# One gate for the tensor engine's visits to half-height tiles in a two-mixer decoder layer

## The chip, the cores and the metric

The kernel runs on one core of a Trainium2 chip. The metric is the device time of one execution in microseconds; the kernel before took a median of 434.82 us in 3 runs (434.67 to 434.88). Lower is better. TensorE (PE) multiplies matrices, VectorE (DVE) and ScalarE (ACT) work elementwise, GpSimd (POOL) does a few adds, SyncE (SP) starts the transfers.

## The reference

One decoder layer on 512 tokens of width 1024. One input projection gives the inputs of two mixers, A (attention with three branches) and B (a gated linear recurrence of 4 heads); their outputs go through gates, two branch projections, an output projection and a layer norm:

```python
h = x @ w_in[l] + b_in[l]
(q_a, kv_a, g_nsa, z_a, q_b, f_b, i_b, z_b, gm_a, gm_b) = jnp.split(h, SPLIT_POINTS, axis=-1)
o_a = nsa_attention(q_a, k_cmp, v_cmp, k_slc, v_slc, k_win, v_win, g_nsa, ...)
o_a = o_a * jax.nn.silu(z_a)
o_b = hgrn2(q_b, f_b, i_b, lb_all[l])
...
y = jax.nn.sigmoid(gm_a) * (o_a @ w_branch_a[l]) + jax.nn.sigmoid(gm_b) * (o_b @ w_branch_b[l])
x = layer_norm(alpha * x + y @ w_out[l], ln_g[l], ln_b[l])
```

In the attention, per block of 128 queries: a branch on 31 compressed blocks, a branch on selected blocks (here all 8 blocks of 64 keys are selected, so it is causal attention on its own keys), and a window branch (512 wide, so again causal attention on its own keys). There are 8 query heads of 64 dimensions in 2 groups that share keys and values.

## The kernel before, in words

**Precision.** Every large product is made of three float32r products of split operands (hi x hi, hi x lo, lo x hi); `split2` (L153) makes the pair: ACT casts to the high part (L154), DVE subtracts to get the low part (L155).

**The long stream.** `proj` (L266) computes a 128-column tile of the input projection: 24 matmuls of 128x512 on a PSUM bank `pa`, from weight tiles `wraw` that are split into `whi` and `wlo` two tiles ahead. Before every sixth matmul it calls `weave.tick()`.

**The weave.** All the rest (recurrence, rotary keys and queries, the attention) is written as generators that run inside the ticks (`_Weave`, L74): a chain yields the number of ticks after which it goes on. `T.matmul`, `T.transpose` and the transfers keep program order, so the order in which the chains issue is the order on PE; a scheduler places ACT's and DVE's instructions. The table `D` (L70) holds the numbers of ticks.

**The attention of the selected and window branches.** `units` (L617) are (query block i, branches): (3, selected), (3, window), (2, selected), (2, window), (1, both), (0, both). For each unit `attn_scores` (L620) makes the scores of one head pair m at a time: the contraction is over 64 dimensions, so two matmuls run on the two halves of 64 rows of PE, each pair into two `pss` banks, three pairs per head pair (hi/lo). Then DVE adds the mask and takes the row maximum (L646), ACT exponentiates with the sum (L649). After four head pairs come reciprocals, gates and the multiplications of the probabilities (L661 on ACT, L663 on DVE). `attn_values` (L667) transposes the probabilities of the unit before, 16 transposes on half tiles of 64 rows into two `pst` banks, splits them (L154, L155) and issues the products with the values (four matmuls into `pso`) of the step before.

A **visit** below is a stretch of PE's order on half-height tiles between matmuls on all 128 rows: scores, transposes, or both in the same tick. Both chains start their visits on even ticks (L631 and L702):

```python
while weave.now % 2:
    yield 1
```

There are two banks each of `pa`, `pss`, `pst` and `pso`. The compressed branch uses `pst` for its transposes (`transpose4`, L595 and L612) and four banks, two of them `pst`, for its products with the values (L675, tiles of 32 rows). `hgrn` (L370) is the recurrence of one head; D["h6"] stands between its state update (L425, L428) and its output matmuls into `pso` (L431).

Of the kernel before, what the change touches and what calls it, by code (L numbers as in the profile page):

```python
# [12 lines left out]
AF = mybir.ActivationFunctionType  # L13
# [36 lines left out]
def _columns(name):  # L50

    c = np.arange(_COLS[name], _COLS[name] + 128)
    if name[0] == "q" and name[1] != "b" or name[:2] == "za":
# [13 lines left out]
    0, 128, 256, 384, 388, 900, 1412, 1924, 2436)  # L67


D = dict(h0=8, h2=4, h3=6, h4=2, h5=8, h6=5, n0=3, n1=2, n2=10, c0=1, c1=6, c2=7, c3=7,  # L70
         r0=5, p0=4, p1=11, p2=2, b0=1, a0=1, a1=1, a3=2, a4=2, a5=1, s0=18, s2=0, s3=1, a6=2)


class _Weave:  # L74


    def __init__(self):
        self.now, self.runs = 0, []

    def start(self, chain, delay=0):  # L80
        self.runs.append([chain, self.now + delay])
# [1 line left out]
    def tick(self):  # L83
        for run in list(self.runs):
            if run[1] <= self.now:
                wait = next(run[0], None)
                if wait is None:
                    self.runs.remove(run)
                else:
                    run[1] = self.now + wait  # L90
        self.now += 1

    def drain(self):
# [5 lines left out]
def layer_kernel(ctx: ExitStack, tc: tile.TileContext, xT, xn, w0, wi, wf, wv, small, brow, consts,  # L99
# [517 lines left out]
    units = [(i, brs) for i in range(3, -1, -1) for brs in (((0,), (1,)) if i >= 2 else ((0, 1),))]  # L617
    probs, pv_at = {}, [0]

    def attn_scores():  # L620
        while not {"keys0", "keys1", "gates"} <= ready or len(QAB) < 4:
            yield 1
        for u, (i, brs) in enumerate(units):
            while u - pv_at[0] > 1:
                yield 1
            n, nb = 128 * (i + 1), len(brs)
            mn, den, ts = SM(8 * nb, "mn"), SM(8 * nb, "dn"), ([], [])
            for m in range(4):
                while weave.now % 2:
                    yield 1  # L630

                pg = PS(), PS()
                qh, ql = (t[:, 128 * i:128 * i + 128] for t in QAB[m])
                for s, (q, k) in enumerate(((qh, KH), (qh, KL), (ql, KH))):
                    for ab in range(2):
                        r = slice(64 * ab, 64 * ab + 64)
                        if nb == 1:
                            dst, kk = pg[ab][:, 0:n], k[r, brs[0], 0:n]
                        else:
                            dst, kk = pg[ab][:, 0:2 * n].rearrange("p (b k) -> p b k", b=2), k[r, :, 0:n]  # L640
                        T.matmul(dst, q[r], kk, start=s == 0, stop=s == 2)
                for ab in range(2):
                    p = T2()
                    for x in range(nb):
                        c, k = slice(n * x, n * x + n), slice(4 * nb * ab + nb * m + x, 4 * nb * ab + nb * m + x + 1)
                        V.tensor_tensor_reduce(out=p[:, c], in0=pg[ab][:, c], in1=amask[:, 512 - n:512],  # L646
                                               op0=ALU.add, op1=ALU.min, scale=-0.125, scalar=3.0e38,
                                               accum_out=mn[:, k])
                        A.activation(p[:, c], p[:, c], AF.Exp, bias=mn[:, k], scale=-1.0, accum_out=den[:, k])  # L649
                    ts[ab].append(p)  # L650
                yield D["a6"]
            yield D["a0"]
            V.reciprocal(den, den)
            den3 = den.rearrange("p (h b) -> p h b", b=nb)
            V.tensor_tensor(den3, den3, gv[:, i, :, 1 + brs[0]:1 + brs[0] + nb], ALU.mult)
            for ab in range(2):
                for m in range(4):
                    for x in range(nb):
                        c, k = slice(n * x, n * x + n), slice(4 * nb * ab + nb * m + x, 4 * nb * ab + nb * m + x + 1)
                        if m % 2:  # L660
                            A.mul(ts[ab][m][:, c], ts[ab][m][:, c], den[:, k])  # L661
                        else:
                            V.tensor_scalar(ts[ab][m][:, c], ts[ab][m][:, c], den[:, k], None, ALU.mult)  # L663
                probs[u, ab] = ts[ab]

    def attn_values():
# [15 lines left out]
        for u, (i, brs) in enumerate(units):  # L682
            n, last = 128 * (i + 1), None
            while (u, 1) not in probs or len(vts) < 4:
                yield 1
            if brs[0] == 0:
                acc = PO(), PO()
                yield D["a1"]

            def products():  # L690

# [5 lines left out]
                        T.matmul(acc[ab], v, pts[k][:, ab], start=brs[x] == 0 and j == 0 and k == 0,  # L697
                                 stop=brs[x] == 1 and j == i and k == 1)

            for x in range(len(brs)):  # L700
                for j in range(i + 1):
                    while weave.now % 2:  # L702
                        yield 1


                    k = slice(n * x + 128 * j, n * x + 128 * j + 128)
                    pq = PT(), PT()
                    for ab in range(2):
# [9 lines left out]
                    if last:  # L718
                        products()
                    last = x, j, pts  # L720
                    yield D["a3"]
            pv_at[0] = u + 1
# [312 lines left out]
```

## Time and profile before

| what | value |
|---|---|
| median of 3 runs | 434.82 us |
| the profiled execution's own time | 435.02 us |
| its span in the trace | 432.9 us |
| PE matmul busy | 423.8 us (98%), 2381 instructions |
| DVE busy, ACT busy | 286.2 us (66%), 238.9 us (55%) |
| the chain that ended last | PE 91%, ACT 5%, DVE 2% |

The profiled execution is 0.20 us above the median. Matmuls are pipelined, so PE's busy share does not say how fast it goes: the distance between the starts of rows does. In a timeline row `x2` or `x16` counts matmuls of one form in a row, and "[0.27 <-ACT t L661]" is idle time before a row and what ended it.

### The profile page before, as it was taken

To read this page: it belongs to the slowest core of one execution; us is meant where nothing else is said; L and a number is where in the kernel's file an instruction comes from. 1 tells how busy PE (TensorE), PEld (TensorE's weight loads), DVE (VectorE), ACT (ScalarE), POOL (GpSimd) and SP (SyncE) were. 2 spreads that over 40 slices of the span, in tenths; PEclk is the share of its full clock that TensorE was granted. 3 is DMA by queue.
4 is the path that set the end of the run, shared out by engine and by line. 5 is a ranking of instruction groups with operands and counts; after the bars stand their busy time and mean duration, and the time that the engine had idled before them with its cause. 6 is when DMAs were issued, how large, how long until landed. Compare 5 with 4: busy or idle time off the path is not lost.

```text
span 432.9 us, 6424 instructions
## 1 busy us (share of the span) xinstructions
PE 423.8 (98%) x2381; PEld 344.8 (80%) x2381; DVE 286.2 (66%) x586; ACT 238.9 (55%) x484; POOL 15.6 (4%) x26
## 2 busy tenths in 40 slices
PE   8999999999999999999999999999999999999994
PEld 7888888888898878867677777776787888888884
DVE  5915669995556476955576556568664797872674
ACT  3534632623437345658777577769676875528300
POOL 2000000000001310000000010001000100000000
PEclk9999999999999999999999999999999999999999
DMA  8995400352420644321111211111252631153031
GB/s 263 393 374 185 166 1 2 85 145 86 123 76 3 188 145 151 97 99 51 48 50 56 81 59 51 51 48 50 73 192 82 218 106 62 50 149 144 15 130 48
DMA packets 20879, 47.58 MB, mean 110 GB/s; under 512 B 2929, under 2 KB 4593, under 8 KB 20849
## 3 DMA queue, kind: packets, MB, share of 16 engines
q1 hardware_dynamic: 20560, 46.92, 33.1%
q8 instruction: 18, 0.29, 0.3%
q10 hardware_dynamic: 288, 0.26, 0.2%
q14 instruction: 13, 0.10, 0.1%
HBM read 41.93 MB, written 2.10 MB: 102 GB/s over the span
## 4 chain that ended last, share of the span: by engine, by line
PE 91%; ACT 5%; DVE 2%; DMA 1%; issue 0%; DVEq 0%; ACTq 0%
PE pa L107 57%; PE pss L107 16%; PE pso L107 12%; PE pst L107 3%; PE pst L111 3%; ACT t L649 2%; ACT t L661 1%; ACT whi L154 1%; DMA t<-in_w_dram 1%; DVE t L155 1%; DVE wlo L155 1%; ACT asum L679 0%; DVE t L646 0%; ACT t L873 0%; ACT t L729 0%; ACT t L154 0%
## 5 line engine op out<-in xcount | busy, mean ns | idle before, releaser
L107 PE MATMUL pa<-t,whi 128*128 128x512 f32 x640 | 200.3, 394 | 0.0
L107 PEld LDWEIGHTS pa<-t,whi 128*128 128x128 f32 x640 | 118.2, 188 | 28.4 <-issue 3.1
L107 PE MATMUL pa<-t,wlo 128*128 128x512 f32 x320 | 124.9, 390 | 0.0
L155 DVE TENSOR_TENSOR wlo<-wraw,whi 128x1024 fp32r<-128x1024 f32 x46 | 56.5, 1231 | 41.0 <-ACT whi L154 41.0
L154 ACT CAST whi<-wraw 128x1024 fp32r<-128x1024 f32 x46 | 48.1, 1048 | 43.9 <-PE pa L107 27.9
L107 PEld LDWEIGHTS pa<-t,wlo 128*128 128x128 f32 x320 | 60.1, 188 | 12.8
L649 ACT ACTIVATE t<-t,sm_mn 128x512 f32<-128x512 f32 (+3 forms) x64 | 35.4, 555 | 26.6 <-DVE sm_mn L646 26.6
L107 PE MATMUL pa<-t,t 128*128 128x512 f32 (+1 forms) x168 | 36.7, 375 | 0.0
L155 DVE TENSOR_TENSOR t<-pst,t 128x512 fp32r<-128x512 f32 x40 | 25.9, 685 | 14.5 <-ACT t L154 14.5
L646 DVE CUSTOM_DVE_ANT_0 t<-pss,t 128x512 f32<-128x512 f32 (+3 forms) x64 | 28.4, 486 | 10.6 <-PE pss L107 8.9
L107 PEld LDWEIGHTS pa<-t,t 128*128 128x128 f32 x168 | 30.3, 188 | 5.6
L107 PE MATMUL pss<-t,t 128*128 128x512 f32 (+3 forms) x222 | 34.5, 310 | 0.0
L107 PE MATMUL pso<-t,t 128*128 128x512 f32 (+2 forms) x158 | 32.9, 343 | 0.2 <-DVE t L188 0.2
L107 PEld LDWEIGHTS pss<-t,t 128*128 128x128 f32 (+1 forms) x222 | 27.5, 175 | 3.7 <-issue 0.7
L107 PEld LDWEIGHTS pso<-t,t 128*128 128x128 f32 x158 | 25.2, 189 | 4.3 <-ACT t L187 0.5
L155 DVE TENSOR_TENSOR t<-t,t 128x512 fp32r<-128x512 f32 (+1 forms) x26 | 17.0, 669 | 16.4 <-ACT t L154 16.4
L154 ACT CAST t<-t 128x512 fp32r<-128x512 f32 (+1 forms) x26 | 15.2, 605 | 22.2 <-DVE t L901 14.8
L107 PE MATMUL pso<-t,vv 128*128 128x512 f32 x80 | 23.7, 417 | 0.0
L111 PEld LDWEIGHTS pst<-con,t 64*128 64x128 f32 (+1 forms) x349 | 16.8, 138 | 6.5 <-DVE t L155 1.7
L154 ACT CAST t<-pst 128x512 fp32r<-128x512 f32 x40 | 21.2, 577 | 0.7 <-PE pst L111 0.6
L111 PE MATMUL pst<-con,t 64*128 64x64 f32 (+1 forms) x349 | 19.6, 229 | 1.7 <-DVE t L663 0.8
L107 PE MATMUL pss<-t,whi 128*128 128x512 f32 x64 | 19.7, 389 | 0.0
(164 smaller groups left out, 501.0 us busy)
## 6 DMA issues: line engine op xcount, KB each, us to landing
wraw<-in_wf_dram SPq DMA_DIRECT2D x38, 512.0 KB, 3.7
wraw<-in_wbr_dram SPq DMA_DIRECT2D x8, 512.0 KB, 3.8
t<-in_wout_dram SPq DMA_DIRECT2D x16, 256.0 KB, 3.4
t<-in_w_dram SPq DMA_DIRECT2D x15, 256.0 KB, 5.6
t<-t SPq DMA_DIRECT2D x48, 64.0 KB, 2.0
t<-in_wi_dram SPq DMA_DIRECT2D x8, 256.0 KB, 6.0
t<-in_xn_dram SPq DMA_DIRECT2D x8, 256.0 KB, 6.6
out_dram<-t SPq DMA_DIRECT2D x8, 256.0 KB, 2.1
```

Of the source, the lines that this page charges most:

```text
L107: return tc.keep_in_program_order(nc.tensor.matmul(*a, **k))
L111: return tc.keep_in_program_order(nc.tensor.transpose(*a, **k))
L154: A.copy(dst_hi, src)
L155: V.tensor_tensor(dst_lo, src, dst_hi.bitcast(F32), ALU.subtract)
L646: V.tensor_tensor_reduce(out=p[:, c], in0=pg[ab][:, c], in1=amask[:, 512 - n:512], op0=ALU.add, op1=ALU.min, scale=-0.125, scalar=3.0e38, ...
L649: A.activation(p[:, c], p[:, c], AF.Exp, bias=mn[:, k], scale=-1.0, accum_out=den[:, k])
L661: A.mul(ts[ab][m][:, c], ts[ab][m][:, c], den[:, k])
```

## The change

One gate, `visit(i)`, replaces the even ticks: a visit may start where the last one started in the same tick, or `D["v%d" % i]` ticks after it (3, 2, 3 and 4 ticks for query blocks 3, 2, 1 and 0). The first unit issues two head pairs per visit, the second pair into `pst` banks. A unit's first scores may start one unit earlier than before. Mask and exponential of a visit are put off to the end of the tick (`late`), behind what the transposes issue. The last unit's two steps of transposes are issued in one visit, the second into `pss` banks. Several delays of `D` become shorter, among them h6 (5 to 4).

```diff
-         r0=5, p0=4, p1=11, p2=2, b0=1, a0=1, a1=1, a3=2, a4=2, a5=1, s0=18, s2=0, s3=1, a6=2)
+         r0=5, p0=4, p1=11, p2=2, b0=2, a0=1, a1=1, a3=1, a4=1, a5=1, s0=18, s2=0, s3=1, a6=1, v0=4, v1=3, v2=2, v3=3)
...
                     run[1] = self.now + wait
+        for work in self.late:
+            work()
+        self.late.clear()
         self.now += 1
...
+    slot = [-1, 0]
+
+    def visit(i):
+        if weave.now != slot[0] and weave.now < slot[1]:
+            return False
+        slot[:] = weave.now, weave.now + D["v%d" % i]
+        return True
...
-            while u - pv_at[0] > 1:
-                yield 1
-            for m in range(4):
-                while weave.now % 2:
-                    yield 1
-                pg = PS(), PS()
+            for ms in ((0, 1), (2, 3)) if u == 0 else ((0,), (1,), (2,), (3,)):
+                while u - pv_at[0] > 1 + (ms[0] == 0) or not visit(i):
+                    yield 1
+                for z, m in enumerate(ms):
+                    if i or z == 0:
+                        pg = (PS(), PS()) if z == 0 else (PT(), PT())
...
+                def masked(ms=ms, dsts=dsts, mn=mn, den=den, ts=ts, n=n, nb=nb):
...
+                weave.late.append(masked)
+                yield D["a6"] * len(ms)
...
-            for x in range(len(brs)):
-                for j in range(i + 1):
-                    while weave.now % 2:
-                        yield 1
+            steps = [(x, j) for x in range(len(brs)) for j in range(i + 1)]
+            for at in (steps,) if i == 0 else [[s] for s in steps]:
+                while not visit(i):
+                    yield 1
+                done = []
+                for x, j in at:
...
-                    pq = PT(), PT()
+                    pq = (PS(), PS()) if done else (PT(), PT())
...
+                    done.append((x, j, pq))
+                if last:
+                    products()
+                for x, j, pq in done:
+                    if x and i == 0:
+                        products()
```

In PE's order the number of matmuls stays the same. Between the first scores and the last transposes the visits change as follows (counted in the two orders):

| kind of visit | before | after |
|---|---|---|
| scores of two head pairs | 0 | 2 |
| scores of one head pair, alone | 8 | 3 |
| transposes alone, 16 | 4 | 1 |
| transposes alone, 32 | 0 | 1 |
| scores and 16 transposes | 16 | 17 |
| the 32-row products | 1 (behind a scores visit) | 1 (by itself) |
| all | 29 | 25 |

Of the 17 combined visits after, 2 are followed by 12 matmuls on `pa` before the next visit, 4 by 12 and four products on `pso`, 3 by 18, and 8 by 18 and four or eight products. Before, 12 lay between most.

**PE, first scores of the attention.** `kh` and `kl` are the split keys, `con` holds the identity of the transposes (here those of the compressed branch). Before:

```order
L107 MATMUL pss<-kh,t_1269 128x512 x2
L107 MATMUL pss<-kl,t_1269 128x512 x2
L107 MATMUL pss<-kh,t_1270 128x512 x2
L107 MATMUL pa<-t_218,whi 128x512
L107 MATMUL pa<-t_219,whi 128x512
L107 MATMUL pa<-t_218,wlo 128x512
L107 MATMUL pa<-t_242,whi 128x512
L107 MATMUL pa<-t_243,whi 128x512
L107 MATMUL pa<-t_242,wlo 128x512
L111 MATMUL pst<-con,t_1677 128x128 x4
L107 MATMUL pa<-t_266,whi 128x512
L107 MATMUL pa<-t_267,whi 128x512
```

After (line numbers are 3 higher there):

```order
L110 MATMUL pss<-kh,t_1269 128x512 x2
L110 MATMUL pss<-kl,t_1269 128x512 x2
L110 MATMUL pss<-kh,t_1270 128x512 x2
L110 MATMUL pst<-kh,t_1355 128x512 x2
L110 MATMUL pst<-kl,t_1355 128x512 x2
L110 MATMUL pst<-kh,t_1356 128x512 x2
L110 MATMUL pa<-t_218,whi 128x512
L110 MATMUL pa<-t_219,whi 128x512
L110 MATMUL pa<-t_218,wlo 128x512
L110 MATMUL pa<-t_242,whi 128x512
L110 MATMUL pa<-t_243,whi 128x512
L110 MATMUL pa<-t_242,wlo 128x512
```

The second pair of scores, which stood behind the transposes and six more `pa` matmuls, now follows the first pair directly, in `pst`; the transposes into the same two banks still come after six `pa` matmuls. The second such visit, after:

```order
L110 MATMUL pa<-t_105,whi 128x512
L110 MATMUL pa<-t_106,whi 128x512
L110 MATMUL pa<-t_105,wlo 128x512
L110 MATMUL pa<-t_145,whi 128x512
L110 MATMUL pa<-t_146,whi 128x512
L110 MATMUL pa<-t_145,wlo 128x512
L110 MATMUL pss<-kh,t_1572 128x512 x2
L110 MATMUL pss<-kl,t_1572 128x512 x2
L110 MATMUL pss<-kh,t_1573 128x512 x2
L110 MATMUL pst<-kh,t_1692 128x512 x2
L110 MATMUL pst<-kl,t_1692 128x512 x2
L110 MATMUL pst<-kh,t_1693 128x512 x2
```

It follows the compressed branch's last transposes by six `pa` matmuls and takes the banks that these filled.

**ACT, first transposes of the attention.** L649 (after: L667) are the exponentials, the casts from `pst` are the copies of the transposes, L873 (after: L900) evacuates `pa`. Before:

```order
L649 ACTIVATE t_2043,sm_dn<-t_2043,sm_mn 128x512
L649 ACTIVATE t_2046,sm_dn<-t_2046,sm_mn 128x512
L154 CAST t_2067<-pst 128x8x64 x2
L649 ACTIVATE t_2093,sm_dn<-t_2093,sm_mn 128x512
L649 ACTIVATE t_2096,sm_dn<-t_2096,sm_mn 128x512
L154 CAST t_2117<-pst 128x8x64 x2
L154 CAST whi<-wraw 128x1024
L873 ACTIVATE t_2139<-pa,hbias 128x512
```

After:

```order
L667 ACTIVATE t_2066,sm_dn<-t_2066,sm_mn 128x512
L157 CAST t_2060<-pst 128x8x64 x2
L667 ACTIVATE t_2069,sm_dn<-t_2069,sm_mn 128x512
L900 ACTIVATE t_2078<-pa,hbias 128x512
L157 CAST whi<-wraw 128x1024
L667 ACTIVATE t_2135,sm_dn<-t_2135,sm_mn 128x512
L157 CAST t_2129<-pst 128x8x64 x2
L667 ACTIVATE t_2138,sm_dn<-t_2138,sm_mn 128x512
```

The two casts of a visit stood behind both exponentials of that visit and now stand ahead of the second. DVE at the same visits, after (L664 ISA is the mask, L158 from `pst` the subtractions):

```order
L664 ISA t_2066,sm_mn<-pss,t_319 128x512
L664 ISA sm_mn 128x1
L664 ISA t_2069,sm_mn<-pss,t_319 128x512
L664 ISA sm_mn 128x1
L158 TENSOR_TENSOR t_2061<-pst,t_2060 128x8x64 x2
L158 TENSOR_TENSOR wlo<-wraw,whi 128x1024
L664 ISA t_2135,sm_mn<-pss,t_319 128x512
L664 ISA sm_mn 128x1
```

On DVE the masks of the visit still stand ahead of the subtractions.

**PE, last transposes.** Before, the last 16, preceded by `pa` matmuls that part them from the 16 before:

```order
L107 MATMUL pa<-t_169,wlo 128x512
L107 MATMUL pa<-t_193,whi 128x512
L107 MATMUL pa<-t_194,whi 128x512
L107 MATMUL pa<-t_193,wlo 128x512
L111 MATMUL pst<-con,t_3077 128x64 x2
L111 MATMUL pst<-con,t_3131 128x64 x2
L111 MATMUL pst<-con,t_3198 128x64 x2
L111 MATMUL pst<-con,t_3256 128x64 x2
L111 MATMUL pst<-con,t_3082 128x64 x2
L111 MATMUL pst<-con,t_3136 128x64 x2
L111 MATMUL pst<-con,t_3203 128x64 x2
L111 MATMUL pst<-con,t_3261 128x64 x2
```

After, the last rows of the first 16 and the second 16:

```order
L114 MATMUL pst<-con,t_3059 128x64 x2
L114 MATMUL pst<-con,t_3136 128x64 x2
L114 MATMUL pst<-con,t_3209 128x64 x2
L114 MATMUL pst<-con,t_3282 128x64 x2
L114 MATMUL pss<-con,t_3054 128x64 x2
L114 MATMUL pss<-con,t_3131 128x64 x2
L114 MATMUL pss<-con,t_3204 128x64 x2
L114 MATMUL pss<-con,t_3277 128x64 x2
L114 MATMUL pss<-con,t_3059 128x64 x2
L114 MATMUL pss<-con,t_3136 128x64 x2
L114 MATMUL pss<-con,t_3209 128x64 x2
L114 MATMUL pss<-con,t_3282 128x64 x2
```

Both sets now stand together, the second in `pss` banks.

## Rows read from the trace of the kernel before

**Rows 1.** the page, parts 2 and 4: granted clock by slice, chain of waits

```profile
PEclk9999999999999999999999999999999999999999
...
PE 91%; ACT 5%; DVE 2%; DMA 1%; issue 0%; DVEq 0%; ACTq 0%
```

**Rows 2.** timeline of PE, 273 to 281 us (start, us, engine line op tiles)

```profile
273.92 0.50 PE L107 MATMUL pss<-kh,t 64*128 64x512 f32 x2
...
274.82 1.19 PE L107 MATMUL pso<-t,vv 128*128 128x512 f32 x4
275.94 0.71 PE L111 MATMUL pst<-con,t 64*128 64x64 f32 x16
276.58 0.72 PE L107 MATMUL pa<-t,whi 128*128 128x512 f32 x2
...
278.07 0.62 PE L107 MATMUL pa<-t,whi 128*128 128x512 f32 x2
...
278.76 0.62 PE L107 MATMUL pa<-t,whi 128*128 128x512 f32 x2
...
279.54 0.50 PE L107 MATMUL pss<-kh,t 64*128 64x512 f32 x2
...
280.93 0.97 PE L107 MATMUL pso<-t,vv 128*128 128x512 f32 x3
```

**Rows 3.** timeline of PE at the visits that stood still, and one that did not

```profile
198.13 0.50 PE L107 MATMUL pss<-kh,t 64*128 64x512 f32 x2
...
204.69 0.50 PE L107 MATMUL pss<-kh,t 64*128 64x512 f32 x2
...
206.47 0.28 PE L111 MATMUL pst<-con,t 64*128 64x64 f32 x2 [0.27 <-ACT t L661]
206.68 0.73 PE L107 MATMUL pa<-t,whi 128*128 128x512 f32 x2
...
209.62 0.50 PE L107 MATMUL pss<-kh,t 64*128 64x512 f32 x2
...
211.83 1.19 PE L107 MATMUL pso<-t,vv 128*128 128x512 f32 x4
...
290.05 0.50 PE L107 MATMUL pss<-kh,t 64*128 64x512 f32 x2
...
297.57 0.39 PE L107 MATMUL pss<-kh,t 64*128 64x256 f32 x2
...
298.73 0.34 PE L111 MATMUL pst<-con,t 64*128 64x64 f32 x4 [0.41 <-DVE t L663]
...
300.05 0.73 PE L107 MATMUL pa<-t,whi 128*128 128x512 f32 x2
...
302.99 0.39 PE L107 MATMUL pss<-kh,t 64*128 64x256 f32 x2
...
304.79 1.20 PE L107 MATMUL pso<-t,vv 128*128 128x512 f32 x4
...
308.65 0.39 PE L107 MATMUL pss<-kh,t 64*128 64x256 f32 x2
...
309.70 1.20 PE L107 MATMUL pso<-t,vv 128*128 128x512 f32 x4
```

**Rows 4.** timelines of PE, ACT and DVE, banks of transposes emptied

```profile
189.85 0.66 PE L111 MATMUL pst<-con,t 128*128 128x128 f32 x4
...
192.54 0.57 ACT L614 COPY t<-pst 128x512 f32<-128x512 f32 x1
...
209.25 1.05 ACT L154 CAST t<-pst 128x512 fp32r<-128x512 f32 x2
...
211.06 0.68 DVE L646 CUSTOM_DVE_ANT_0 t<-pss,t 128x512 f32<-128x512 f32 x1
```

**Rows 5.** timelines of DVE and PE, output of one recurrence head

```profile
105.41 0.73 DVE L428 SCALAR_TENSOR_TENSOR t<-t,sm_dlab,pss 128x128 f32<-128x128 f32 x2
...
112.10 1.16 PE L107 MATMUL pso<-t,t 128*128 128x128 f32 x9
```

More of the change, by code (lines that the diff above doesn't have):

```diff
@@ L67 @@
     0, 128, 256, 384, 388, 900, 1412, 1924, 2436)
-D = dict(h0=8, h2=4, h3=6, h4=2, h5=8, h6=5, n0=3, n1=2, n2=10, c0=1, c1=6, c2=7, c3=7,
-         r0=5, p0=4, p1=11, p2=2, b0=1, a0=1, a1=1, a3=2, a4=2, a5=1, s0=18, s2=0, s3=1, a6=2)
+D = dict(h0=8, h2=4, h3=6, h4=2, h5=8, h6=4, n0=3, n1=2, n2=10, c0=1, c1=6, c2=7, c3=7,
+         r0=5, p0=4, p1=11, p2=2, b0=2, a0=1, a1=1, a3=1, a4=1, a5=1, s0=18, s2=0, s3=1, a6=1, v0=4, v1=3, v2=2, v3=3)
 class _Weave:
     def __init__(self):
-        self.now, self.runs = 0, []
+        self.now, self.runs, self.late = 0, [], []
     def start(self, chain, delay=0):
@@ L623, in attn_scores @@
         for u, (i, brs) in enumerate(units):
-            while u - pv_at[0] > 1:
-                yield 1
             n, nb = 128 * (i + 1), len(brs)
             mn, den, ts = SM(8 * nb, "mn"), SM(8 * nb, "dn"), ([], [])
-            for m in range(4):
-                while weave.now % 2:
+            for ms in ((0, 1), (2, 3)) if u == 0 else ((0,), (1,), (2,), (3,)):
+                while u - pv_at[0] > 1 + (ms[0] == 0) or not visit(i):
                     yield 1
-                pg = PS(), PS()
[L633 to L651, printed above, removed]
@@ new lines, in attn_scores @@
+                dsts = {}
+                for z, m in enumerate(ms):
+                    if i or z == 0:
+                        pg = (PS(), PS()) if z == 0 else (PT(), PT())
+                    qh, ql = (t[:, 128 * i:128 * i + 128] for t in QAB[m])
+                    for s, (q, k) in enumerate(((qh, KH), (qh, KL), (ql, KH))):
+                        for ab in range(2):
+                            r = slice(64 * ab, 64 * ab + 64)
+                            d = dsts[m, ab] = pg[ab][:, 256 * z * (i == 0):][:, 0:nb * n]
+                            if nb == 1:
+                                kk = k[r, brs[0], 0:n]
+                            else:
+                                d, kk = d.rearrange("p (b k) -> p b k", b=2), k[r, :, 0:n]
+                            T.matmul(d, q[r], kk, start=s == 0, stop=s == 2)
@@ new lines, in masked @@
+                def masked(ms=ms, dsts=dsts, mn=mn, den=den, ts=ts, n=n, nb=nb):
+                    for m in ms:
+                        for ab in range(2):
+                            p = T2()
+                            for x in range(nb):
+                                c, h = slice(n * x, n * x + n), 4 * nb * ab + nb * m + x
+                                V.tensor_tensor_reduce(out=p[:, c], in0=dsts[m, ab][:, c], in1=amask[:, 512 - n:512],
+                                                       op0=ALU.add, op1=ALU.min, scale=-0.125, scalar=3.0e38,
+                                                       accum_out=mn[:, h:h + 1])
+                                A.activation(p[:, c], p[:, c], AF.Exp, bias=mn[:, h:h + 1], scale=-1.0,
+                                             accum_out=den[:, h:h + 1])
+                            ts[ab].append(p)
@@ L685, in attn_values @@
                 yield 1
+            yield D["a1"]
             if brs[0] == 0:
                 acc = PO(), PO()
-                yield D["a1"]
             def products():
@@ L717, in attn_values @@
                                *(t.rearrange("p b (m h q) -> p (b m) h q", m=4, h=2)[:, :, h] for t in pts))
-                    if last:
-                        products()
                     last = x, j, pts
```

## The prediction

> **What bounds the kernel now.** I read the chain of waits first: PE holds 91% of it [rows 1], so time is won only by what shortens PE's own row of work. The clock by slice is 9 in all forty slices [rows 1], so no slice is slow because of the clock. PE's busy share says nothing more, and I went to its timeline, to be read by the distance from start to start. In the long stream three 128x512 matmuls take 0.69 us (278.07 to 278.76) [rows 2]. A visit to half tiles costs more than its matmuls. Scores alone, 273.92 to 274.82, take 0.90 us; sixteen transposes alone, 275.94 to 276.58, take 0.64; the two together, 279.54 to 280.93, take 1.39 [rows 2]: 0.15 less than apart. The twelve stream matmuls between two visits, 276.58 to 279.54, take 2.96 where twelve steady ones take 2.76 [rows 2]: 0.20 for going out and back. One visit spared is thus worth 0.35 us. Second, four visits stand still in the middle. Scores with transposes should take 1.39 us in the first two units and 1.05 (308.65 to 309.70) in the last one [rows 3]. Taken were 1.99 (204.69 to 206.68), 2.21 (209.62 to 211.83), 2.48 (297.57 to 300.05) and 1.80 (302.99 to 304.79) [rows 3].
>
> **The change part by part.** *Fewer visits.* The table in the change has 29 before and 25 after.
> - First unit: four visits of one head pair become two of two head pairs. A double visit is not in this trace; three more pairs of 512 columns go at the stream's step, 3 x 0.23 = 0.69, so 0.90 + 0.69 = 1.59. Two merges spare (2 x 0.90 - 1.59) + 0.20 = 0.41 each, 0.82.
> - Last unit: 16 more transposes inside a visit cost 1.39 - 0.90 = 0.49, so 32 take 0.64 + 0.49 = 1.13, and the merge spares 0.15 + 0.20 = 0.35.
> - One lone scores visit and one lone visit of transposes become one: 0.35.
> - The 32-row products stood directly behind scores and now need their own way out and back: 0.20 lost.
>
> Together 1.3 us. Bounds: 0.6 if the four merges spare the way alone (4 x 0.20 - 0.20), 1.8 if a double visit also spares the 0.15 and the 32-row products' way costs nothing.
>
> [...] The rows show 0.35 for one visit, so the measurement decides, and the sum goes by it.
>
> *The stalls.* They are 1.99 - 1.39 = 0.60, 2.21 - 1.39 = 0.82, 2.48 - 1.05 = 1.43 and 1.80 - 1.05 = 0.75: 3.60 us. I take each in turn.
> 1. At 206.47 PE waited for ACT's last multiplication of the first unit's probabilities [rows 3]. From the start of the last scores visit, 198.13, to there are 8.3 us. After, the last scores are a double visit, which adds two exponentials on ACT. Behind it stand 12 stream matmuls, the 32-row products, 6, one lone scores visit and 18: 1.59 + 2.96 + (at least 0.5) + 1.6 + 0.90 + 4.3 = 11.9 us. Two more exponentials do not take the 3.6 us to spare. Gone.
> 2. At 209.62 the transposes found their banks full: the casts that empty them started on ACT only at 209.25 [rows 4], 2.6 us after the transposes' visit had ended. In between ACT had that visit's two exponentials, a weight cast and an evacuation. After, the first of these visits is followed by 18 stream matmuls (4.3 us) in place of 12, the multiplications are long done, and the casts stand ahead of the second exponential in ACT's order. Gone.
> 3. At 298.73 the transposes waited for DVE's multiplications (L663) of the fifth unit [rows 3]; from its last scores, 290.05, to the end of that visit, 300.05, are 10.0 us. After, 1.39 + 0.92 + 2.96 + 0.5 (the last unit's first scores, alone) + 0.92 + 5.7 = 12.4 us lie between, of which that visit's own casts and subtractions, now beside its masks, take some 2. Gone, but with little to spare.
> 4. At 302.99 the banks were full again, as a consequence of 3. After, 18 lie between and nothing is late. Gone.
>
> Bounds: all of the 3.60, or none if they only move.
>
> *Banks shared at the start.* The double visits take the `pst` banks of the compressed branch's transposes. The second such visit comes after four transposes (0.4), six stream matmuls (1.5) and its own first half (0.8): 2.7 us after those transposes start. Before, that bank was emptied at 192.54 + 0.57 = 193.11, 3.3 us after 189.85 [rows 4], but behind an exponential that itself waited; after, only a weight cast and two evacuations stand ahead. Ends 0 and 0.6; I take 0.1, near the lower one, since the exponential is gone from the queue. The masks free the other hand-overs in time by a few tenths. [...]
>
> *Masks put off.* On DVE the masks still stand ahead of the subtractions in the order, so the score banks come free as before: nothing, if the order holds; the price if not is the third rival.
>
> *h6.* The recurrence's output matmuls go one tick earlier (six stream matmuls and what lies between, 1.4 to 2 us). For one head their operand was ready at 105.41 + 0.73 = 106.14 and they began at 112.10 [rows 5]. The six microseconds between cover it: nothing. Without cover it would be at most 2 us for each of four heads.
>
> *Transfers.* One weight load on SP stands behind four more small copies; its tile is used two tiles (some 11 us of stream) after its split: nothing.
>
> *Sum.* -1.3 - 3.6 + 0.1 = -4.8 us against the profiled execution's own 435.02: 430.2. That execution was 0.20 above the median of 434.82, so the median should be **430.0 us**.
>
> **The rivals.**
> - *Banks as the new wait.* At the three hand-overs of `pst` in the first unit (double visit to transposes, transposes to double visit, double visit to 32-row products) PE waits for DVE or ACT, up to the 0.6 of above each, 1.8 in all: 431.8 in place of 430.1 or so. For it speaks the copy at 192.54 [rows 4]; against it the shorter queue ahead of that copy. [...] The rows show such a wait before only for transposes, at 209.62.
> - *The stalls only move.* ACT and DVE keep their work, and where units meet it comes in bunches of eight multiplications. If the spare time of 3 is used up and others open, only the visits' part is left: 434.82 - 1.3 + 0.1 = 433.6. Against it: the distances grew by 2 to 4 us at each place.
> - *Slower: masks that hold the score banks.* If DVE in fact masks after the copies, the second score bank of a combined visit comes free 1.39 + w + 1.8 + 1.3 = 4.5 us + w after the visit's start, w being how late the casts start. 1.8 is the stretch from the first cast (209.25) to the mask behind the subtractions (211.06) [rows 4], and 1.3 are two masks of 0.68. The next visit comes after 4.35 us (12 between, 2 visits), 5.3 (4 visits), 5.7 (3) or 6.6 (8). With w = 2.6 as at 209.25 the stalls are 2 x 2.75 + 4 x 1.8 + 3 x 1.4 + 8 x 0.5 = 21 us; if casts are so late at every second visit, half of it: 430.0 + 10.5 = 440.5. It decides from w of some 1.3 at every visit, where it has eaten the 4.8. Against it stands DVE's order in the change, and that casts stand earlier on ACT.
>
> **How the numbers follow.** The forecast has 0.73; banks 0.12; moved stalls 0.10; slower 0.05. A measurement can tell 0.2%, 0.9 us, from no change. Faster by more holds in the forecast, the banks' case and most of the moved stalls (433.6 lies 1.2 below): 0.92; the same 0.04; slower 0.04. The range: below, 1.8 for the visits, all stalls and no new wait, 434.82 - 5.4 = 429.4, and a little for the shapes not in the trace: 429.2. Above it takes in the banks' case, 431.8, and leaves out what lies over 432.0.
>
> **What would show it.** In the profile after: 25 visits; a double visit of 1.6 us and one of 32 transposes of 1.1; no row on PE between the first scores and the last transposes with idle time of more than 0.1 us ahead of it; PE's busy share no higher. A wait of PE on `pst` in the first unit (released by a copy or a mask) would be the first rival; waits for multiplications where units meet the second; waits of `pss` matmuls on the mask line the third. Wrong altogether would be a total above 434.

## The result and the profile after

The changed kernel took a median of **430.59 us** (430.23 to 430.67, 5 runs) against 434.82 (434.14 to 434.92, 5 runs) for the kernel before in the same measurement: ratio 0.9905, 95% interval 0.9890 to 0.9919, 4.2 us less. The forecast was 430.0, its range 429.2 to 432.0. Measured once more with the experiments below, the changed kernel took 430.55 us (ratio 0.9904, 0.9890 to 0.9917).

| what | before | after |
|---|---|---|
| the profiled execution's own time, span | 435.02, 432.9 us | 430.23, 428.3 us |
| PE matmul busy | 423.8 us (98%) | 421.1 us (98%) |
| chain: PE, ACT, DVE | 91%, 5%, 2% | 98%, 0%, 1% |
| first scores to the end of the last transposes | 184.64 to 329.12: 144.48 us | 184.10 to 324.50: 140.40 us |
| visits in that stretch | 29 | 25 |

The page of the changed kernel, part 4 (chain of waits), and the whole list of PE's waits (waiting matmuls, what released them, us in total, times, longest):

```profile
PE 98%; DVE 1%; DVEq 0%; issue 0%; ACT 0%
```

```profile
PE pso L110 <- DVE t L169: 1.1, 1, 1.1
```

ACT's 5% are gone from the chain of [rows 1]: the only wait that the list names lies at the program's start. PE's timeline of the changed kernel, at the places that answer to [rows 3] and at the new shapes (start, us, engine line op tiles):

```profile
184.10 0.50 PE L110 MATMUL pss<-kh,t 64*128 64x512 f32 x2
...
185.69 0.50 PE L110 MATMUL pa<-t,whi 128*128 128x512 f32 x1
...
190.92 0.51 PE L110 MATMUL pss<-kh,t 64*128 64x512 f32 x2
...
192.76 0.50 PE L110 MATMUL pa<-t,whi 128*128 128x512 f32 x1
...
203.53 0.50 PE L110 MATMUL pss<-kh,t 64*128 64x512 f32 x2
...
204.92 0.50 PE L110 MATMUL pa<-t,whi 128*128 128x512 f32 x1
...
209.24 0.50 PE L110 MATMUL pss<-kh,t 64*128 64x512 f32 x2
...
210.62 0.50 PE L110 MATMUL pso<-t,vv 128*128 128x512 f32 x1
...
280.42 1.04 PE L110 MATMUL pss<-kh,t 64*128 64x512 f32 x2
...
282.35 0.50 PE L110 MATMUL pso<-t,vv 128*128 128x512 f32 x1
...
298.60 0.38 PE L110 MATMUL pss<-kh,t 64*128 64x256 f32 x2
...
299.65 0.72 PE L110 MATMUL pa<-t,whi 128*128 128x512 f32 x2
...
303.97 0.38 PE L110 MATMUL pss<-kh,t 64*128 64x256 f32 x2
...
305.02 0.50 PE L110 MATMUL pso<-t,vv 128*128 128x512 f32 x1
...
323.36 0.71 PE L114 MATMUL pst<-con,t 64*128 64x64 f32 x16
...
324.50 0.73 PE L110 MATMUL pa<-t,whi 128*128 128x512 f32 x2
```

Read by the distance from start to start: the four visits that stood still in [rows 3] now take 1.39 (203.53), 1.38 (209.24), 1.05 (298.60) and 1.05 us (303.97); all four stalls are gone. The first double visit takes 1.59, the one of 32 transposes 1.14 (323.36 to 324.50). Two visits are longer than their shape: the second double visit, 1.84 (190.92 to 192.76, 0.25 too long), and the one at 280.42, 1.93 (0.55 too long). The list of waits does not show them; they show in the distances alone, the second one also in the 1.04 us of its first pair.

The stretch holds the same matmuls in both kernels, among them 384 of the stream and 72 of the products, so the two lengths can be compared. In it: 3.61 of stalls gone, 0.80 of new waits; what is left of the 4.08 us won, 4.08 - 3.61 + 0.80 = 1.27, is the visits'. The spans differ by 0.5 more because the first scores came 0.54 earlier. That is no more than traces of one order differ by: in nine traces whose programs are alike up to there (the changed kernel twice, and e1 to e5, e7 and e8 below) the first scores start anywhere from 183.60 to 184.93. So stretches are compared below, and totals only where they differ by more.

What held the two places? ACT of the changed kernel around the second double visit and ahead of 280.42, then DVE there (in brackets the idle time before a row and what ended it):

```profile
189.14 1.05 ACT L157 CAST whi<-wraw 128x1024 fp32r<-128x1024 f32 x1
190.09 0.69 ACT L846 ACTIVATE t<-pa,sml 128x512 f32<-128x512 f32 x1
190.67 0.68 ACT L848 ACTIVATE t<-pa,hbias 128x512 f32<-128x512 f32 x1
191.24 0.58 ACT L617 COPY t<-pst 128x512 f32<-128x512 f32 x1
...
275.98 1.05 ACT L157 CAST whi<-wraw 128x1024 fp32r<-128x1024 f32 x1 [1.81 <-PE pa L110]
```

```profile
277.06 1.23 DVE L158 TENSOR_TENSOR wlo<-wraw,whi 128x1024 fp32r<-128x1024 f32 x1 [3.97 <-ACT whi L157]
278.20 0.42 DVE L664 CUSTOM_DVE_ANT_0 t<-pss,t 128x256 f32<-128x256 f32 x1
...
279.23 1.28 DVE L158 TENSOR_TENSOR t<-pst,t 128x512 fp32r<-128x512 f32 x2
280.43 0.41 DVE L664 CUSTOM_DVE_ANT_0 t<-pss,t 128x256 f32<-128x256 f32 x1
```

The copy that frees the `pst` bank ended at 191.82, behind a weight cast and two evacuations; the second half of the double visit was due 0.80 us after its start, as in the first double visit (184.10 to 184.90), at 191.72, and waited for it. At 280.42 the fourth mask of the visit before stood on DVE behind both subtractions, ended at 280.84, and its score bank was not free. DVE had stood still for 3.97 us, though, with a weight subtraction first in its line, which waited for the cast at 275.98, and that one had waited 1.81 us for PE's matmuls. Which of the two holds the bank, the order or the weight subtraction, the rows alone don't say.

### The profile page after: what moved, and what is told of

Same layout as the page of the kernel before. It is cut to its first block, busy times and chain, and to the rows that moved or that the text cites. A ratio compares the mean times of both kernels' runs of the same rounds, so it can differ in the third digit from the quotient of the medians.

```text
span 428.3 us, 6417 instructions
## 1 busy us (share of the span) xinstructions
PE 421.1 (98%) x2381; PEld 344.9 (81%) x2381; DVE 287.5 (67%) x586; ACT 239.1 (56%) x484; POOL 14.8 (3%) x26
## 4 chain that ended last, share of the span: by engine, by line
PE 98%; DVE 1%; DVEq 0%; issue 0%; ACT 0%
PE pa L110 62%; PE pss L110 16%; PE pso L110 13%; PE pst L110 4%; PE pst L114 3%; DVE t L979 0%; DVEq L1058 0%; PE pss L114 0%; DVE sm_bst L967 0%; DVE t L966 0%; ACT sm_rs L974 0%; DVE sm_ag L971 0%; DVE t L169 0%; DVE sm_rs L975 0%
## 5 line engine op out<-in xcount | busy, mean ns | idle before, releaser
L158 DVE TENSOR_TENSOR wlo<-wraw,whi 128x1024 fp32r<-128x1024 f32 x46 | 56.6, 1232 | 42.4 <-ACT whi L157 41.2
L667 ACT ACTIVATE t<-t,sm_mn 128x512 f32<-128x512 f32 (+3 forms) x64 | 35.7, 559 | 24.5 <-DVE sm_mn L664 24.4
L664 DVE CUSTOM_DVE_ANT_0 t<-pss,t 128x384 f32<-128x384 f32 (+3 forms) x60 | 26.1, 473 | 13.3 <-PE pss L110 13.3
L158 DVE TENSOR_TENSOR t<-pst,t 128x512 fp32r<-128x512 f32 x38 | 24.5, 685 | 9.1 <-ACT t L157 9.1
L158 DVE TENSOR_TENSOR t<-t,t 128x512 fp32r<-128x512 f32 (+1 forms) x26 | 17.6, 689 | 15.1 <-ACT t L157 15.0
L157 ACT CAST t<-pst 128x512 fp32r<-128x512 f32 x38 | 20.1, 579 | 0.3 <-PE pst L114 0.3
L110 PE MATMUL pss<-kh,t 64*128 64x512 f32 (+2 forms) x88 | 18.2, 401 | 0.1
```

The source lines that it names most:

```text
L110: return tc.keep_in_program_order(nc.tensor.matmul(*a, **k))
L157: A.copy(dst_hi, src)
L158: V.tensor_tensor(dst_lo, src, dst_hi.bitcast(F32), ALU.subtract)
L664: V.tensor_tensor_reduce(out=p[:, c], in0=dsts[m, ab][:, c], in1=amask[:, 512 - n:512], op0=ALU.add, op1=ALU.min, scale=-0.125, scalar=3.0e38,
L667: A.activation(p[:, c], p[:, c], AF.Exp, bias=mn[:, h:h + 1], scale=-1.0, accum_out=den[:, h:h + 1])
```

## The experiments

They ran in three groups; the kernel before took 434.55, 434.74 and 434.69 us beside them. In the diffs - and + are against the changed kernel, and `...` stands for what is left out.

**e1_first_single: what two visits cost.**

```diff
-            for ms in ((0, 1), (2, 3)) if u == 0 else ((0,), (1,), (2,), (3,)):
+            for ms in ((0,), (1,), (2,), (3,)):
...
-            yield D["a1"]
+            yield D["a1"] + 1 * (u == 0)
```

> The changed kernel, but the first unit's scores go one head pair at a time again (27 visits in place of 25; one delay is two visits' worth longer for the first unit only, so that its transposes still come 18 stream matmuls behind one more lone scores visit). Theory (a visit costs 0.2 us for the way out and back and 0.2 us for its own beginning): two visits more, 2 x 0.41 = +0.82 us, and the 0.25 us that the second double visit waited for its pst banks goes: 430.59 + 0.57 = 431.2 us. [...] In the trace the theory wants 0.90 us for each single visit against 1.59 for a double one, and 0.20 us extra in each stretch of stream matmuls between two visits.

Measured 432.72 us (ratio 0.9954, 0.9942 to 0.9966). The shapes are as the theory has them: single visits of 0.90, 0.90, 0.90 and 0.89 us, 3.59 in all, against 2 x 1.59 = 3.18 for two double ones, and some 0.2 us of way out and back in each stretch between. The wait on `pst` is gone. But the total is 1.5 us longer than expected, and the reason lies elsewhere: everything behind comes later, the last transposes end at 333.29, and the last unit's products now stand still. PE's timeline of this kernel:

```profile
335.29 0.50 PE L110 MATMUL pso<-t,vv 128*128 128x512 f32 x1 [0.34 <-ACT t L157]
336.90 0.96 PE L110 MATMUL pso<-t,vv 128*128 128x512 f32 x3 [1.10 <-DVE t L158]
```

By distances these two waits are 0.51 and 1.38 us, and the 0.55 us of 280.42 does not occur. From the first scores to PE's last matmul the kernel takes 240.20 us, the changed one (its second trace, e11 below) 238.11: 0.81 - 0.25 - 0.55 + 1.89 = 1.90 of the 2.09 are named. The price of a visit stands, the total was forecast wrong, because a visit more also moves what follows against ACT and DVE.

**e2_first_single_close: is it the distance that cures the first stall?** As e1, without the second edit.

> As e1_first_single (27 visits too), without the longer delay: the first unit's transposes come 18 stream matmuls after its last scores, without a lone visit between. Theory (the stalls at the start of a unit are the time from its last scores to its last multiplication, 8.3 us in the kernel before, less the time that PE has work between): the transposes would start 0.90 + 4.30 + 0.90 = 6.1 us after those scores, so about 2 us of standing still (1.5 to 2.5) in that visit, and the kernel 1.5 to 2.5 us slower than e1_first_single: 432.7 to 433.7 us. Rival (the stalls before came from the order on ACT, which is as after here, not from the distance): no wait there, the same time as e1_first_single.

Measured 432.38 us (ratio 0.9947, 0.9935 to 0.9959). The wait is there, with the releaser of [rows 3], ACT's multiplications:

```profile
208.81 0.34 PE L114 MATMUL pst<-con,t 64*128 64x64 f32 x4 [0.21 <-ACT t L682]
209.42 0.28 PE L114 MATMUL pst<-con,t 64*128 64x64 f32 x2 [0.27 <-ACT t L682]
```

That visit takes 2.30 in place of 1.39 us, 0.91 too long; in e1, with 5.2 us more between, the same visit takes 1.39. So the mechanism holds, at half the size: the 8.3 us from last scores to last multiplication are not a constant; here they were 7.3 (202.14 to 209.42). I had expected it to be 1.5 to 2.5 us slower than e1. It is not, since e1 loses 1.89 at its end and this one 0.66 there.

**e3_last_apart: one visit more, nothing else.**

```diff
-            for at in (steps,) if i == 0 else [[s] for s in steps]:
+            for at in [[s] for s in steps]:
...
-                    if x and i == 0:
+                    if x and i == 0 and len(done) > 1:
```

> The changed kernel, but the last unit's two sets of 16 transposes are two visits again, 24 stream matmuls apart (26 visits). Theory: 0.15 us for a second beginning and 0.20 us for a second way out and back: 430.59 + 0.35 = 430.95 us, and 0.64 us for each visit against 1.14 for the one of 32. [...]

```profile
324.20 0.71 PE L114 MATMUL pst<-con,t 64*128 64x64 f32 x16
324.84 0.73 PE L110 MATMUL pa<-t,whi 128*128 128x512 f32 x2
...
330.49 0.71 PE L114 MATMUL pst<-con,t 64*128 64x64 f32 x16
331.13 0.50 PE L110 MATMUL pso<-t,vv 128*128 128x512 f32 x1
```

Measured 430.73 us (430.56 to 431.66; ratio 0.9914, 0.9901 to 0.9927), 0.14 to 0.18 above the changed kernel, less than a measurement can tell. The trace can: 0.64 us for each visit of 16 where 32 in one take 1.14, and 5.65 us for the 24 stream matmuls between, where 24 steady ones would take 5.44 (18 of them, 325.63 to 329.71 in this trace, take 4.08). From the first scores to PE's last matmul it is 238.47 us against 238.11: 0.36 for one visit. The theory had 0.35.

**e4_masks_behind: the slower rival made to happen.**

```diff
-                                V.tensor_tensor_reduce(...)
+                                tc.keep_in_program_order(V.tensor_tensor_reduce(...))
...
-                        split2(pq[h].rearrange(...), *(...))
+                        src = pq[h].rearrange(...)
+                        hi, lo = (...)
+                        A.copy(hi, src)
+                        tc.keep_in_program_order(V.tensor_tensor(lo, src, hi.bitcast(F32), ALU.subtract))
```

> The changed kernel, but on DVE the masks of a combined visit are held behind the subtractions that empty the transposes' banks, so the score banks come free later; all else stays. This is the mechanism of the slower rival, made to happen. Theory: the casts are no longer late after the change, so the score banks come free in time wherever 18 or more matmuls follow, and only the visits that 12 follow stand still, each by 0.3 to 1 us: 2 to 4 us in all, 432.5 to 434.5 us. Rival (as priced in the prediction: casts 2.6 us late at every second visit): about 10 us, 440. In the trace: waits of pss matmuls on the mask.

Measured 432.74 us (ratio 0.9959, 0.9947 to 0.9971): 2.15 us slower, inside the theory's 2 to 4 and far from 10. The stretch is 142.85 us against 140.40. But the largest piece is at a place that neither had named, the products. PE and DVE of this kernel:

```profile
228.61 0.97 PE L110 MATMUL pso<-t,vv 128*128 128x512 f32 x3 [0.74 <-DVE t L749]
```

```profile
226.13 1.23 DVE L158 TENSOR_TENSOR wlo<-wraw,whi 128x1024 fp32r<-128x1024 f32 x1 [2.49 <-ACT whi L157]
```

The subtractions that make the products' operands (L749 there) ran only from 227.27, behind a weight subtraction that had waited 2.49 us first in line: 1.0 us by distance. A second products' wait cost 0.24 (ahead of 256.90). Score banks, the cost that the theory and the rival are about, cost 0.65 (292.91, behind a visit that 12 stream matmuls follow) and 0.38 (300.70, behind one that 24 follow), 1.03 in all. So the total fell inside the theory's range in part by luck. The rival's 10 us also presume casts that come 2.6 us late; in the changed kernel they start 0.1 to 1.5 us after the end of their combined visit (the latest at 225.13, after 223.67).

**e5_masks_at_once and e6_before_masks_late: which part cured which stall.** e5 is the changed kernel with `masked()` called where it is defined:

```diff
-                weave.late.append(masked)
+                masked()
```

> The changed kernel, but mask and exponential are issued with the scores again and not put off to the end of the tick; TensorE's order, its 25 visits and their distances stay. So all four masks of a visit stand ahead of the subtractions on DVE, and two exponentials ahead of the casts on ACT. Theory: the four stalls went by the distance between visits, so they stay away; the 0.55 us at 280.42, where the fourth mask stood behind the two subtractions, goes: 430.0 us (429.9 to 430.8, the upper end if a visit with 12 matmuls behind it now finds its transposes' banks full). Rival (it was the casts' place ahead of the second exponential that removed the second and fourth stall): 0.8 + 0.75 come back, 431.4 to 432.2 us.

e6 is the kernel before with the same `masked` function and `late` list put in, and its table, gates and visits as they were.

> The kernel before with one part of the change alone: mask and exponential put off to the end of the tick. TensorE's order is that of before, 29 visits. Theory: the first and third stall (0.60 and 1.43) are waits for multiplications and stay within a few tenths, since nothing was put between; the second (0.82) and fourth (0.75) are banks waiting for casts that stood behind exponentials and shrink to 0.3 or less each: 1.0 to 1.5 us less, 433.3 to 433.8. Rival (distance alone counts): 434.6, no change. Other rival (the order alone counts): all four go, 3.6 less, 431.0.

e6 took 433.14 us (ratio 0.9966, 0.9957 to 0.9976), 1.6 less than the kernel before beside it; its stretch is 143.04 us, 1.44 less. PE's timeline of e6 at the four places:

```profile
206.15 0.28 PE L114 MATMUL pst<-con,t 64*128 64x64 f32 x2 [0.27 <-ACT t L666]
...
209.30 0.50 PE L110 MATMUL pss<-kh,t 64*128 64x512 f32 x2
...
210.76 0.50 PE L110 MATMUL pso<-t,vv 128*128 128x512 f32 x1
...
297.71 0.34 PE L114 MATMUL pst<-con,t 64*128 64x64 f32 x4 [0.41 <-DVE t L668]
...
301.97 0.38 PE L110 MATMUL pss<-kh,t 64*128 64x256 f32 x2
...
303.02 1.20 PE L110 MATMUL pso<-t,vv 128*128 128x512 f32 x4
```

ACT's casts ahead of the second place:

```profile
207.51 1.06 ACT L157 CAST t<-pst 128x512 fp32r<-128x512 f32 x2
```

The waits for multiplications (first and third) stand as in [rows 3]; they take 1.99 and 2.48 us. The second visit takes 1.46 in place of 2.21, the fourth 1.05 in place of 1.80: the casts that started at 209.25 in [rows 4] start at 207.51, ahead of both exponentials of their visit. So the casts' place ahead of the exponentials is nearly or wholly enough for the second and fourth stall, and does nothing for the first and third. e5 took 431.07 us (430.40 to 431.38; ratio 0.9916, 0.9902 to 0.9930), its stretch 140.90, 0.50 more than the changed kernel's, and there none of the four came back (1.38, 1.39, 1.04 and 1.11 us): with masks and exponentials issued at once, as before the change, the distance is enough for all four. The second and fourth were cured twice over. What in the distance comes from the gate, what from the shorter delays and what from the scores that start a unit earlier was not tried apart. The wait at 280.42 did not go as I had expected. With all four masks ahead, the subtractions were late instead. PE's and DVE's rows:

```profile
282.52 0.71 PE L114 MATMUL pst<-con,t 64*128 64x64 f32 x15 [0.56 <-DVE t L158]
```

```profile
281.77 0.69 DVE L158 TENSOR_TENSOR t<-pst,t 128x512 fp32r<-128x512 f32 x1 [0.99 <-ACT t L157]
```

That visit takes 2.21 us, 0.83 too long in place of 0.55. The second subtraction waited 0.99 us for its cast, which ACT ran from 281.18, behind all four exponentials. So the fourth mask's place alone was not the cause: with it moved ahead, another bank was late.

**e7_all_three_ticks: more distance.**

```diff
-... v0=4, v1=3, v2=2, v3=3)
+... v0=4, v1=3, v2=3, v3=3)
```

> The changed kernel with the distance of block 2's visits at 3 ticks in place of 2 (18 stream matmuls between all visits of blocks 3 to 1; 24 visits, since one lone visit of transposes merges with scores). Theory: the wait of 0.55 us at 280.42, score banks that the fourth mask had not yet freed behind a visit with 12 matmuls after it, goes, and one visit less spares 0.35: 430.59 - 0.9 = 429.7 us. Rival (the fourth mask is late for a reason of its own, the weight subtraction ahead of it on DVE that waits for ACT): the wait moves to another visit, 430.2 us.

Measured 435.06 us (ratio 1.0010, 1.0000 to 1.0021), against an expectation of 429.7. The visit in question is clean (1.38 us at 280.46), but the last unit's first scores now merge with the transposes of the unit before, and the lone visit whose matmuls lay between the fifth unit's last scores and its transposes is gone. PE's timeline:

```profile
301.22 0.34 PE L114 MATMUL pst<-con,t 64*128 64x64 f32 x4 [0.40 <-ACT t L682]
...
330.26 0.50 PE L110 MATMUL pso<-t,vv 128*128 128x512 f32 x1 [1.13 <-ACT t L157]
331.87 1.65 PE L110 MATMUL pso<-t,vv 128*128 128x512 f32 x3 [1.10 <-DVE t L158]
```

The visit with the fifth unit's transposes starts 5.2 us after the one with its last scores (294.65 to 299.89) and takes 1.29 too long, a stall at the third one's place, this time behind ACT's multiplications and not DVE's. The last products are late as in e1 (1.9): from the end of the last transposes, 327.48, the products and the stream matmuls up to 336.99 take 9.51 us, where the changed kernel takes 5.17 for the same ones (324.50 to 329.67), 4.3 us more. The expectation had counted one visit saved and not what lay in it as cover.

**e8_copy_on_dve: the 0.25 us at the second double visit.**

```diff
-        A.copy(PTc[g], ps)
+        (V.tensor_copy if g else A.copy)(PTc[g], ps)
```

> The changed kernel, but the second compressed branch's transposes are copied out of their bank by DVE in place of ACT, where three instructions stood ahead of the copy. Theory: the second double visit takes 1.59 us again in place of 1.84, and nothing else moves: 430.59 - 0.25 = 430.3 us. Rival (the bank is late whoever copies it, or DVE's own queue holds it): 430.6 or more, and PE's wait at 190.9 to 192.8 is then released by DVE.

Measured 431.01 us (430.02 to 431.59; ratio 0.9916, 0.9901 to 0.9931), and the rival was right: the visit takes 2.07 us, longer than 1.84, and the stretch 140.66, 0.26 more. The copy now stands on DVE behind the subtraction of the same weights:

```profile
189.72 1.23 DVE L158 TENSOR_TENSOR wlo<-wraw,whi 128x1024 fp32r<-128x1024 f32 x1 [2.59 <-ACT whi L157]
190.86 0.68 DVE L617 COPY t<-pst 128x512 f32<-128x512 f32 x1
```

**e9_weight_lo_on_pool and e10_four_whi: is it the weight subtraction first in line?**

```diff
-            split2(raws[i], hi, lo)
+            A.copy(hi, raws[i])
+            (G if 17 <= i < 36 else V).tensor_tensor(lo, raws[i], hi.bitcast(F32), ALU.subtract)
```

> The changed kernel, but for the 19 weight tiles used during the attention and after it the subtraction that makes wlo (1.23 us on DVE) is done by POOL; TensorE's order stays. Theory: the 0.55 us at 280.42 came from DVE's first in line, a weight subtraction that waited 3.97 us for ACT's cast while the masks and subtractions of the visit stood behind it; without it the masks start as soon as the scores are there, the fourth one is done in time and the wait goes; the 0.25 at 190.92 stood on ACT and stays: 430.59 - 0.55 = 430.0 us. POOL's subtraction should take about 2.5 us (twice its 128x512 of 1.28) and is not in any way. Rival (DVE has too much to do between those two visits, whatever stands first): the wait stays, 430.6 us. Rival (POOL's work slows DVE or comes too late for TensorE): slower than 431.

```diff
+    strh = ctx.enter_context(tc.tile_pool(name="strh", bufs=4))
-    t2 = ctx.enter_context(tc.tile_pool(name="t2", bufs=63))
+    t2 = ctx.enter_context(tc.tile_pool(name="t2", bufs=61))
...
-            hi = strm.tile([P, 1024], F32R, name="whi", tag="whi")
+            hi = strh.tile([P, 1024], F32R, name="whi", tag="whi")
```

> The changed kernel with four buffers for whi in place of three (and 61 in place of 63 of the common tiles, to make room); TensorE's order stays. Theory: the cast of whi that held ACT's line (at 275.98 it had waited 1.81 us for TensorE to give up its buffer) runs earlier, the weight subtraction on DVE then waits only for its own buffer, the masks of that visit start about 1.1 us earlier, and the 0.55 us at 280.42 goes: 430.0 us, or 429.8 if the copy at 191.24 also moves up. Rival (the wait is made of DVE's own work): 430.6 us. Two tiles fewer could make a new wait on the common pool, which would show as late work on ACT or DVE.

> The changed kernel itself, unaltered, beside the two others on the same chip: what a trace differs by with nothing changed. Expected 430.6 us (430.2 to 431.0); the start of the first scores anywhere from 183.6 to 184.9 us as in the traces so far, and the stretch from there to the end of the last transposes 140.40 us within 0.05, with the two waits of 0.25 and 0.55.

e11, the changed kernel again: 430.55 us, stretch 140.39, the two waits 0.24 and 0.54. In both other kernels the visit at 280.42 is clean: 1.39 us in e9 (284.50 to 285.89) and in e10 (280.23 to 281.62). DVE of e10 there:

```profile
276.07 1.22 DVE L159 TENSOR_TENSOR wlo<-wraw,whi 128x1024 fp32r<-128x1024 f32 x1 [3.30 <-issue]
277.21 0.42 DVE L665 CUSTOM_DVE_ANT_0 t<-pss,t 128x256 f32<-128x256 f32 x1
...
279.27 1.29 DVE L159 TENSOR_TENSOR t<-pst,t 128x512 fp32r<-128x512 f32 x2 [0.60 <-ACT t L158]
```

The weight subtraction no longer waits for a cast (with a buffer more the cast runs a tile ahead: on ACT a cast of `whi` ran from 275.79 to 276.84, beside this subtraction). DVE still stood 3.30 us with it first in line, for something that the row does not name, but the masks start at 277.21 in place of 278.20, in a trace whose scores came 0.2 earlier, and no bank is late. The order behind it differs too: all four masks stand ahead of the subtractions, as in e5, and on ACT the casts stand behind two exponentials, where e5 has one cast behind all four. So the run alone does not part the start from the order. An estimate from the rows does: with the changed kernel's order and a start 0.8 us earlier, the fourth mask would have ended at 280.04, before 280.42; with e10's order and the changed kernel's start, the subtractions would have ended 3.35 us after 278.20, at 281.55, after the transposes were due (280.42 + 0.81 = 281.23). By this the cause of the 0.55 is when DVE got past the weight subtraction first in its line; that the order behind it counts for nothing is not shown. The 0.25 at the start is as it was (1.85 us at 190.68), so the hope of 429.8 did not come true. e10 took **430.29 us** (429.94 to 430.47; ratio 0.9896, 0.9881 to 0.9911), its stretch is 139.90 us, 0.49 less than e11's. It is the best version found; by median alone (0.26 less than e11) a measurement would hardly tell it. e9 took 433.52 us (ratio 0.9969, 0.9957 to 0.9980), 3 slower, for the reasons in the last section.

## Why the prediction was right

*Fewer visits: -1.3.* Left over in the stretch: 1.27. The new shapes came out as added up from the stream's step: 1.59 for a double visit (forecast 1.59), 1.14 for 32 transposes (1.13), and one visit measured by itself cost 0.36 (e3; forecast 0.35).

*Stalls: -3.60.* Measured 3.61, all four. By cause the prediction was right for the first and third: only the distance removes them (e5 against e6), and taking distance away brings the wait back (e2, e7). For the second I named both the distance and the casts' order, and either alone takes it away but for 0.07 us (e6); for the fourth I named only the distance. I also called the fourth a consequence of the third, and that was wrong: in e6 the third stands at 2.48 us and the fourth is gone. The spare times worked out from start to start were rough: from the last scores to the last multiplication it was 8.3 us in the trace before and 7.3 in e2.

*Banks shared at the start: +0.1.* Measured 0.25 (0.24 in e11), between the ends 0 and 0.6. I took the lower end because an exponential had left the queue ahead of the copy. The weight cast and two evacuations that I saw ahead of it were not timed: they ran from 189.14 to 191.24 without a pause, so the copy ended 2.82 us after its transposes began (189.00), where I had 2.7 to spare. This is the first rival's mechanism at one of its three hand-overs, at about a seventh of its price (0.25 of 1.8).

*Masks put off: 0, "if the order holds".* This is the step that was mis-sized, by 0.55 us. The order held for three masks of the visit at 276.10 and not for the fourth, and the sum priced DVE's order as if DVE were ready to begin. It was not: its first instruction waited 3.97 us for ACT. It is the third rival in small, at a single visit. Made general in e4, it costs 2.45 us of the stretch, 1.03 of them at score banks; the prediction had priced it, with casts 2.6 us late, at some 10.

*h6 and the transfers: 0.* Not tried by themselves. The list of PE's waits has no entry for the recurrence's outputs or for a weight transfer, but it misses short waits. With h6 at 5 (the kernel before and e6) the first scores start at 184.64 and 184.31, inside the 183.60 to 184.93 of the nine traces with 4: no cost is seen, though one of up to a microsecond could hide in that spread.

Together -1.27 - 3.61 + 0.80 = -4.08 us in the stretch, against -4.8 forecast: the 0.7 missing are the new waits, 0.80 in place of 0.1. The median fell by 4.23; the 0.15 beyond the stretch is less than the start of the first scores differs by between traces. The profiled execution came out at 430.23, just on the 430.2 of the sum; that is luck, since 0.54 of its fall is the early start.

## What to carry to other kernels

Where the bounding engine's row has detours of another shape, price a detour from start to start, with the way out and back: such figures held to 0.02 us here. A stall where a result comes late was cured here by work put between (0.60 and 1.43 us), and the same edit elsewhere can take such cover away, so every change of distance has to be followed to the last consumer (e1, 1.89 us at its end; e7, 4.3). Ask first what stands at the head of an engine's line and waits: here the split of a later weight tile, issued before its cast could run, held DVE for 3.97 us with the masks behind it. Neither order of the masks that was tried (the change's and e5's) took the stall away; one more buffer did (e10).

## What the runs showed of the hardware that was not expected

Moving the weight subtractions to POOL (e9) took 19 subtractions of 1.23 us off DVE and made the kernel 3 us slower. DVE by form in the stretch 150 to 330 us, first e9, then e11 (count, busy us, mean ns, idle before):

```profile
L158 DVE TENSOR_TENSOR t<-pst,t 128x512 fp32r<-128x512 f32 x38 | 24.5, 686 | 14.1 <-ACT t L157 14.1
...
L685 DVE TENSOR_SCALAR t<-t,sm_dn 128x384 f32<-128x384 f32 x8 | 5.0, 684 | 0.1
...
L476 DVE SCALAR_TENSOR_TENSOR t<-t,ngh,t 128x512 f32<-128x512 f32 x3 | 5.2, 1739 | 0.0
```

```profile
L158 DVE TENSOR_TENSOR t<-pst,t 128x512 fp32r<-128x512 f32 x38 | 24.5, 686 | 9.2 <-ACT t L157 9.2
...
L684 DVE TENSOR_SCALAR t<-t,sm_dn 128x384 f32<-128x384 f32 x8 | 2.9, 417 | 0.1
...
L475 DVE SCALAR_TENSOR_TENSOR t<-t,ngh,t 128x512 f32<-128x512 f32 x3 | 2.2, 745 | 0.0
```

The subtractions that read a PSUM bank took 686 ns in both; the multiplications of 128x384 within SBUF went from 417 to 684 ns, and three operations with two SBUF operands from 745 to 1739. One of these ran from 179.79 to 182.50, over the end of a POOL subtraction of 2.54 us that had begun at 179.41; on ACT a cast waited 3.21 us for it with two evacuations behind, and PE lost 1.1 us on a `pa` bank at 183.03. Earlier two operations on DVE took 1.82 us (154.74) and 1.77 (157.09) beside POOL's, in place of 0.69 and 0.75, and PE's compressed scores took 2.33 us (from 159.41) in place of e11's 1.02, 1.3 more. Another 0.84 at 206.77 is of a different kind: the mask stood on DVE behind an operation that had waited 2.98 us for ACT. Less the 0.55 gained at 284.50, these come to 2.7 of the 3 us.

The operation at 179.79 took 2.71 us and ended 0.55 after POOL's. Two others did the same: the one at 175.46 took 1.66 us and ended 0.54 after the POOL subtraction of 174.17, the one at 186.46 took 1.83 and ended 0.55 after that of 185.34. Four multiplications of 128x384 from 273.25 took 3.55 us beside POOL's subtraction of 273.75 to 276.26, the other four of the group 1.45 (by the difference from its 5.0). By what means POOL's work and DVE's are tied the rows do not show. A mostly idle POOL (4% busy in the kernel before) was no free place for this work: beside its 2.4 us per tile (POOL's mean was 2413 ns) these operations of DVE took longer.
